# A projection's weight splits, one scan product and one group's transposes moved in the order of a hybrid decoder step

## The chip, the cores and the metric

The kernel runs on one core of one Trainium2 chip. The metric is the device time in microseconds, median over runs; lower is better. Five engines work side by side, each through its own queue in order: PE (matrix products; PEld is its weight load), DVE, ACT and POOL (element work), and SP, which issues nearly all loads.

## The reference, cut to what matters

One decoder layer for 512 prompt tokens and 8 x 8 sample tokens (576 columns), all in fp32:

```
x += 1/2 gate1 * SwiGLU1(mod(rmsnorm(x)))
h  = mod(rmsnorm(x))
x += gate2 * W_out( sum_i sigmoid(gate_i(h)) * proj_i(branch_i(h)) )
     A: dilated window attention, three head groups (dilation 1, 4, 16), merged by softmax denominators
     B: Mamba-2 scan in chunks of 128, conv, gated group norm
     C: RG-LRU with conv, block gates, GeLU side gate
x += 1/2 gate3 * SwiGLU2(mod(rmsnorm(x)));  final rmsnorm
```

Sample tokens attend to cached keys and values (4096 past positions, windows 128, 512, 2048).

## The kernel before, in words

Every dense product is done as three fp32r products of split operands: `xh*wh + xh*wl + xl*wh`, where the high part is a rounding cast (ACT) and the low part the remainder (DVE, or POOL for units made with `pool=True`). The work is a list of **units**, one per 128 output columns. `run` walks them: for each it issues loads ahead on SP (`more(room)`, room counted in products of one half), splits weights ahead on ACT and DVE/POOL (`split`), takes the finished unit before it out of PSUM (`evict`), and issues its matmuls, 24 for a unit with four k tiles and both halves of the columns. `later(n, f)` puts an instruction off by n calls of `flush`; a unit without lanes flushes twice, once at its start ahead of `evict` and once in its middle. Units whose lanes name "sk" or "sv" are `tight`: they load two units ahead at most and split one ahead. Wide tiles come from two pools with a fixed number of buffers, W (17) and B (55); a new tile takes the buffer that was given back longest ago, and its first writer waits for that buffer's last reader. PSUM has four buffers for units (`mm`) and four for everything else (`px`).

**Lanes** are generators that are stepped between a unit's matmuls, by a share per unit, and so fill in the rest: `ssd` (scan), `attn` (prompt attention and merge), `sk` and `sv` (sample keys, sample values), `lru`. A unit can also drain lanes: it runs what is left of them before its own products.

The order around the change: 16 units of branch B gates and others carry `ssd`; 36 q/k/v units carry `attn`; then 16 units of branch C (attn 7 steps a unit, sk 8, sv 4, lru 2), 11 gate units (sk 5, sv 5, lru 4), the 8 units of the C projection (c0 to c7 here: sk 2, sv 5), the 8 units of the A projection (a0 to a7; a0 drains attn, sk and sv and then splits the sample columns of the attention output, `split_o`), and `w_out` (o0 to o7 for the first half of the columns, then again for the second). a0/a1 and o0/o1 are mates: both run all but their last two k tiles first. `ev_proj` (line 2243 on) takes a projection out of PSUM: two products with the sigmoid gate (line 2248), the sum with the branches before (line 2250), and for the A projection a split of the mixed row (`split`, line 191 high on ACT, line 192 low on DVE) for `w_out`. Its gate and sum come back from DRAM (`sg`, `m`, by `ld_proj`).

The scan (`ssd`) works on 20 items (chunk, group of four heads) in a pipeline of turns: stage_a (a product `pb`, line 1387, and ACT), stage_b (ACT exponent), stage_c (line 1412, M times C.B mask on DVE; line 1415 on POOL), stage_d two turns later (products `py`), and beside them a prelude of the next chunk whose parts end in DVE products (`cbm` line 1341, `xd`, `xe` line 1355) and `state`.

Prompt attention (`pattn`) for the third group has four batches: scores (PE, line 1735; DVE adds the bias, takes the maximum), exponents (`expo`, ACT, line 1767), transposes (`transp`, PE, line 1774; copies on ACT and DVE) and `pv` (line 1791). After the three groups `pmerge` makes merge factors, sends them through DRAM (`facd`), loads them back spread out (`fx`), and then sk begins.

Of the kernel before, what the change touches and what calls it, by code (L numbers as in the profile page):

```python
# [140 lines left out]
class Kern:  # L141
# [125 lines left out]
    def run(self, units):  # L267
        nc = self.nc
        raws, wts, pss = {}, {}, {}
        nl = ns = 0  # L270
# [71 lines left out]
        seq = list(range(len(units)))  # L342
# [4 lines left out]
        at, begin = 0, {}  # L347
# [9 lines left out]
        first = self.start(ahead, split)  # L357
        ns = 2
        segs = self.segments(units, first)
        last = {g.i: n for n, g in enumerate(segs)}  # L360
        seen = 0
        for n, g in enumerate(segs):
            i, u = g.i, units[g.i]
            seen = max(seen, i)
            end = begin[seen] + size(units[seen])
            nxt = rank[min(seen + 1, len(units) - 1)]
            early = n < len(first) - 2
            tight = any(name in ("sk", "sv") for name, _ in u.lanes) or "sk" in g.drain or n < len(first)
            def more(room):
                nonlocal nl  # L370
                while nl < len(units) and begin[seq[nl]] < end + room:
                    load(seq[nl])
                    nl += 1

            if tight:
                while nl < len(units) and nl <= seen + 2 and not early:
                    load(nl)
                    nl += 1
            else:
                more(16 if isinstance(u, Pair) else 48 if nl == len(units) or isinstance(units[seq[nl]], Unit) else 32)  # L380
            while ns <= min(nxt, nl - 1) and not early:
                split(seq[ns])
                ns += 1
            self.flush()
            evict()
            for _ in range(0 if tight else 2):
                if ns < nl and begin[seq[ns]] < end + (32 if isinstance(units[seq[ns]], Unit) else 20 if isinstance(u, Unit) else 0):
                    split(seq[ns])
                    ns += 1
            for d in g.drain:  # L390
                self.drain(d)
            if g.pre is not None:
                g.pre()
            if isinstance(u, Pair):
                self.products(u, wts.pop(i), lambda n, most=7: prep(i, n, most), lambda: more(48))
                continue
            ks = u.ks()
            nk = u.w.shape[1]
            if i not in pss:
                pss[i] = {hf: self.mm() for hf in u.halves}  # L400
            (WH, WL), M, ps = wts[i], u.M, pss[i]
            kr = range(nk) if g.kr is None else g.kr
            ev = self.events(g.lanes)
            at = 0
            for q, k in enumerate(kr):
                xh, xl = ks[k]
                if any(e[2] in (id(xl), id(WL)) for e in self.todo):
                    self.flush(True)
                for p, (wt, x) in enumerate(((WH, xh), (WL, xh), (WH, xl))):
                    for hf in g.halves:  # L410
                        nc.tensor.matmul(  # L411
                            ps[hf][:M, :HALF], wt[k] if isinstance(wt, list) else wt[:, k, :], x[:, hf * HALF:(hf + 1) * HALF],
                            start=(k == 0 and p == 0), stop=(k == nk - 1 and p == 2))
                if not ev and q == len(kr) // 2:
                    self.flush()
                if g.mid is not None and q == len(kr) // 2:
                    g.mid()
                if q % 2:
                    prep(i + 2, 4, 1)
                while at < len(ev) and at * len(kr) < (q + 1) * len(ev):  # L420
                    self.flush()
                    self.step(ev[at], 1)
                    at += 1
            if last[i] == n:
                pend.append((u, pss.pop(i)))
                if i not in kept:
                    wts.pop(i)
                if u.share:
                    wts.pop(i - u.share)
# [885 lines left out]
    def ssd(self):  # L1315
# [92 lines left out]
        def stage_c(c, hg):  # L1408
            L, cs, g = (128 if c < 4 else 64), cols(c), hg // 2
            M, cv = st[c, hg]  # L1410
            four = lambda t: t.rearrange("p (h l) -> p h l", h=4)
            nc.vector.tensor_tensor(out=four(M[0:L, 0:4 * L]), in0=four(M[0:L, 0:4 * L]),
                                    in1=ctx[c][1][0:L, g * 128:g * 128 + L].unsqueeze(1).to_broadcast([L, 4, L]), op=ALU.mult)
            if c > 0:
                nc.gpsimd.tensor_tensor(out=four(cv), in0=four(cv), in1=xbc[10 + g][:, cs].unsqueeze(1).to_broadcast([128, 4, L]),
                                        op=ALU.mult)
# [20 lines left out]
        def state(c):  # L1437

            bt, cbm, xd, xe, decb, css = ctx[c]
            Sn = S[c + 1] = self.W([1024], F32, "S")  # L1440
            if c > 0:
                nc.vector.tensor_tensor(out=Sn.rearrange("p (h d) -> p h d", h=16), in0=S[c].rearrange("p (h d) -> p h d", h=16),
                                        in1=decb.unsqueeze(2).to_broadcast([128, 16, 64]), op=ALU.mult)
            for g in range(2):
                pst = self.px("pst")
                nc.tensor.matmul(pst, bt[:, g * 128:(g + 1) * 128], xe[:, g * 512:(g + 1) * 512], start=True, stop=True)
                sv = Sn[:, g * 512:(g + 1) * 512]
                if c == 0:
                    nc.scalar.copy(sv, pst)
                else:  # L1450
                    nc.vector.tensor_tensor(out=sv, in0=sv, in1=pst, op=ALU.add)
# [5 lines left out]
        for n in range(len(items) + 4):  # L1457
            if 0 <= n - 4:
                stage_d(*items[n - 4])
            if 0 <= n - 1 < len(items):  # L1460
                stage_b(*items[n - 1])
            if 0 <= n - 2 < len(items):
                stage_c(*items[n - 2])
            if n < len(items):
                c, hg = items[n]
                if hg == 0:
                    nxt = prelude(c + 1) if c < 4 else None
                    if c < 4:
                        diagonal(c + 1)
                if nxt is not None:  # L1470
                    next(nxt)
                stage_a(c, hg)
                if hg == 0 and c > 0:
                    yield
                    state(c - 1)
            yield

        for q in range(2):
# [223 lines left out]
    def pattn(self, g):  # L1702
# [99 lines left out]
                    nc.vector.tensor_copy(o.rearrange("p (i r) -> p r i", r=r), p.rearrange("p (r i) -> p r i", r=r))  # L1802
                self.po[g, j] = o

        for i in range(nb + 2):
            if 0 <= i - 1 < nb:
                transp(i - 1, 0)
            if i < nb:
                scores(i)
            if 0 <= i - 2 < nb:  # L1810
                pv(i - 2)
            yield
            if 0 <= i - 1 < nb:
                transp(i - 1, 1)
            if i < nb:
                expo(i, 0)
                expo(i, 1)
            yield
# [423 lines left out]
    def ev_proj(self, n, j, first, last):  # L2242
        def f(ps):
            nc = self.nc
            t, m = self.sg.pop((n, j))
            for hf in range(2):
                tv = t[:, hf * HALF:(hf + 1) * HALF]
                nc.vector.tensor_tensor(out=tv, in0=tv, in1=ps[hf][:, :HALF], op=ALU.mult)  # L2248
            if not first:
                nc.vector.tensor_tensor(out=t, in0=m, in1=t, op=ALU.add)  # L2250
            if last:
                self.mix[j] = self.split(t, (1, 2))
            else:
                self.store(self.md[:, j, :], t)
        return f
# [11 lines left out]
    def mixer_units(self):  # L2267
# [7 lines left out]
        u = []  # L2275
# [4 lines left out]
        def proj(w, nk, ks, n, first, last, start, drain, lanes=()):  # L2280
            for j in range(8):
                def pre(j=j):
                    if j == 0:
                        start()
                        self.ld_proj(n, 0, first)
                    if j < 7:
                        self.ld_proj(n, j + 1, first)
                    if last and j > 5:
                        self.ld_x(j - 6)

                def mid(j=j):
                    t = self.sg[n, j][0]
                    self.nc.scalar.activation(t, t, AF.Sigmoid)

                u.append(Unit(self.wview(w, 0, nk, j * 128), ks, self.ev_proj(n, j, first, last), lanes=lanes, mid=mid, pool=last,
                              pre=pre, drain=drain if j == 0 else ()))

        self.zh = {}
        for j in range(4):
# [194 lines left out]
```

## Time and profile before

| | us |
|---|---|
| median of 3 runs | 2040.97 (2040.9 to 2043.84) |
| the profiled execution | 2043.27 |
| its span, first to last instruction | 2041.3 |
| mean granted TensorE clock | 0.988 |
| busy: PE, PEld, DVE, ACT, POOL | 1976.8, 1855.3, 1230.4, 934.0, 246.4 |

The span lies 1.97 us below its execution's time, which is 2.3 us above the median. PE is busy nearly all of the time, so what can be won lies in its few idle stretches and in those that follow them.

### The profile page before, as it was taken

How to read it: one execution, taken by the hardware profiler on the slowest of the kernel's cores; microseconds unless marked ns; L12 is line 12 of the kernel's file. 1: busy time of each engine (PE TensorE's matmuls, PEld its weight loads, DVE VectorE, ACT ScalarE, POOL GpSimd, SP SyncE). 2: the span in 40 equal slices, each digit the busy share in tenths (PEclk: the TensorE clock that was granted, in tenths of full speed). 3: DMA queues.
4: the chain of work that ended last, by engine and by line, in shares of the span. 5: the costliest groups of instructions: out<-in, count | busy, mean ns of one | idle time of the engine just before them, and what ended most of it. 6: DMA issues, size and time to landing. Idle time of an engine off the chain costs nothing.

```text
span 2041.3 us, 40890 instructions
## 1 busy us (share of the span) xinstructions
PE 1976.8 (97%) x16648; PEld 1855.3 (91%) x16648; DVE 1230.4 (60%) x2463; ACT 934.0 (46%) x1885; POOL 246.4 (12%) x339
## 2 busy tenths in 40 slices
PE   7999999999999999999999989999999999999997
PEld 6779999999897899999999878888988899999997
DVE  4848677785768555225453684435345767777783
ACT  5424434356667346125352646556423743424252
POOL 2000000004004211000002131101124500000011
PEclk8999999999999999999999989999999999999998
DMA  9783223254531585332333175887877423323241
GB/s 272 262 270 115 83 83 104 83 135 155 173 102 51 169 242 167 106 111 61 87 95 98 46 248 164 283 274 239 271 247 223 155 63 104 103 80 95 78 135 55
DMA packets 374051, 300.53 MB, mean 147 GB/s; under 512 B 16304, under 2 KB 322085, under 8 KB 373864
## 3 DMA queue, kind: packets, MB, share of 16 engines
q1 hardware_dynamic: 363848, 267.48, 44.1%
q0 software_dynamic: 10016, 30.44, 4.4%
q8 instruction: 131, 2.15, 0.4%
q14 instruction: 56, 0.46, 0.1%
HBM read 266.21 MB, written 31.66 MB: 146 GB/s over the span
## 4 chain that ended last, share of the span: by engine, by line
PE 73%; DVE 10%; issue 7%; ACT 4%; DMA 3%; SPq 1%; POOL 1%; POOLq 0%; DVEq 0%; ACTq 0%
PE mm L411 46%; PE mmd L513 5%; PE mmb L513 4%; PE mmc L513 4%; PE mma L513 2%; PE kt L2019 2%; DVE op L441 2%; SPq L181 1%; PE S L2007 1%; DVE raw L441 1%; PE px_ld L776 1%; DVE wl L316 1%; PE O L2112 1%; DMA ada<-w_ada 1%; PE sc L1735 1%
## 5 line engine op out<-in xcount | busy, mean ns | idle before, releaser
L411 PE MATMUL mm<-H,wh 128*128 128x288 f32 (+1 forms) x2832 | 677.2, 309 | 5.6 <-DVE sg L2248 2.3
L411 PE MATMUL mm<-L,wh 128*128 128x288 f32 (+1 forms) x2832 | 640.2, 296 | 3.9 <-DVE L L192 2.8
L411 PE MATMUL mm<-H,wl 128*128 128x288 f32 (+1 forms) x2832 | 639.5, 296 | 1.3 <-DVE wl L316 0.8
L411 PEld LDWEIGHTS mm<-H,wh 128*128 128x128 f32 (+1 forms) x2832 | 463.6, 189 | 55.5 <-issue 41.6
L411 PEld LDWEIGHTS mm<-L,wh 128*128 128x128 f32 (+1 forms) x2832 | 466.6, 189 | 6.0 <-DVE L L192 3.9
L411 PEld LDWEIGHTS mm<-H,wl 128*128 128x128 f32 (+1 forms) x2832 | 466.4, 189 | 2.5 <-DVE wl L316 1.0
L316 DVE TENSOR_TENSOR wl<-raw,wh 128x1024 fp32r<-128x1024 f32 (+2 forms) x181 | 199.6, 1109 | 128.4 <-ACT wh L314 107.9
L447 ACT CAST op<-raw 128x512 fp32r<-128x512 f32 x228 | 135.2, 620 | 272.0 <-DVE raw L441 226.4
L314 ACT CAST wh<-raw 128x1024 fp32r<-128x1024 f32 (+2 forms) x217 | 200.6, 940 | 29.2 <-PE mm L411 21.2
L441 DVE TENSOR_TENSOR op<-raw,op 128x512 fp32r<-128x512 f32 x228 | 155.4, 686 | 26.3 <-ACT op L447 24.1
L900 DVE SCALAR_TENSOR_TENSOR x<-mm,modT,x 128x288 f32<-128x288 f32 (+1 forms) x144 | 65.0, 479 | 128.6 <-PE mm L411 128.6
L513 PE MATMUL mmd<-H,op 128*128 128x288 f32 x608 | 125.6, 299 | 1.8 <-DVE mmd L496 1.8
L513 PE MATMUL mmb<-H,op 128*128 128x288 f32 x608 | 124.0, 296 | 1.2 <-ACT su L960 1.2
L513 PE MATMUL mmc<-H,op 128*128 128x288 f32 x608 | 123.6, 296 | 0.0
L316 POOL TENSOR_TENSOR wl<-raw,wh 128x1024 fp32r<-128x1024 f32 (+2 forms) x36 | 74.9, 2091 | 401.6 <-ACT wh L314 395.1
L513 PEld LDWEIGHTS mmd<-H,op 128*128 128x128 f32 x608 | 98.5, 190 | 3.4 <-DVE mmd L496 2.3
L513 PEld LDWEIGHTS mmb<-H,op 128*128 128x128 f32 x608 | 97.5, 188 | 3.0 <-ACT su L960 2.1
L513 PEld LDWEIGHTS mmc<-H,op 128*128 128x128 f32 x608 | 97.6, 189 | 2.6 <-ACT u L526 0.8
L513 PE MATMUL mmd<-L,op 128*128 128x288 f32 x304 | 90.2, 297 | 0.0
L513 PE MATMUL mmb<-L,op 128*128 128x288 f32 x304 | 89.8, 295 | 0.0
L513 PE MATMUL mmc<-L,op 128*128 128x288 f32 x304 | 89.5, 295 | 0.0
L2024 ACT COPY KT<-kt 128x512 f32<-128x512 f32 x78 | 45.6, 588 | 75.2 <-PE kt L2019 66.9
(439 smaller groups left out, 2877.0 us busy)
## 6 DMA issues: line engine op xcount, KB each, us to landing
raw<-w_in SPq DMA_DIRECT2D x96, 512.0 KB
raw<-w_ff_in SPq DMA_DIRECT2D x88, 512.0 KB
ada<-w_ada SPq DMA_DIRECT2D x72, 512.0 KB
ck<-cache_win_kv SPq DMA_DIRECT2D x52, 512.0 KB
cv<-cache_win_kv SPq DMA_DIRECT2D x52, 512.0 KB
raw<-w_ff_out SPq DMA_DIRECT2D x60, 384.0 KB
sgd<-sg POOLq DMA_DIRECT2D x24, 288.0 KB, 4.6
sg<-sgd SPq DMA_DIRECT2D x24, 288.0 KB
```

Of the source, the lines that this page charges most:

```text
L181: self.nc.sync.dma_start(out, in_)
L314: nc.scalar.copy(H, r)
L316: self.later(0 if i < 4 else 2, lambda: e.tensor_tensor(out=L, in0=r, in1=H.bitcast(F32), op=ALU.subtract), L)
L411: nc.tensor.matmul(ps[hf][:M, :HALF], wt[k] if isinstance(wt, list) else wt[:, k, :], x[:, hf * HALF:(hf + 1) * HALF], start=(k == 0 and p ...
L441: nc.vector.tensor_tensor(out=o, in0=a, in1=b, op=op)
L447: nc.scalar.copy(ops[k][0], s)
L513: nc.tensor.matmul(banks[bank], wt[:, q, :], m, start=first and q == 0 and p == 0, stop=q == len(xs) - 1 and p == 2, skip_group_check=True)
L776: nc.tensor.matmul(ps[32 * c4:32 * c4 + 32, :], self.cT[:, k, :], r[:, q * 512:(q + 1) * 512], start=(k == 0), stop=(k == 7), skip_group_c ...
L900: nc.vector.scalar_tensor_tensor(out=x[:, c0:c0 + n], in0=ps[hf][:, 0:n], scalar=g[:, 0:1], in1=x[:, c0:c0 + n], op0=ALU.mult, op1=ALU.add)
L1735: nc.tensor.matmul(ps[hh][:, c0:c0 + 128], self.qkv["q", g, j][64 * hh:64 * hh + 64, a * 128:(a + 1) * 128], self.qkv["k", g, j][64 * hh:6 ...
L2019: nc.tensor.transpose(ps[:, j * 128:(j + 1) * 128], t[:, q, j * 128:(j + 1) * 128], self.ident)
L2024: nc.scalar.copy(kt, ps)
```

## The change

Four edits. (1) The A projection's units lose `pool=True` and get `soon = 80`: they are split through the branch of `split` that takes B buffers and puts the low parts on DVE, and `run` loads with a room of `soon + 16` (96, was 48) while the next unit to load has a `soon`, and splits with `soon` in place of 32. (2) The mixed rows' low parts are put off by 3 flushes (was 2). (3) In the scan, stage_c stands behind the prelude's part and stage_a of its turn. (4) In the third attention group transposes and `pv` run one batch later.

```diff
-                more(16 if isinstance(u, Pair) else 48 if nl == len(units) or isinstance(units[seq[nl]], Unit) else 32)
+                more(16 if isinstance(u, Pair) else units[seq[nl]].soon + 16 if nl < len(units) and units[seq[nl]].soon else 48 if nl == len(units) or isinstance(units[seq[nl]], Unit) else 32)
...
-                if ns < nl and begin[seq[ns]] < end + (32 if isinstance(units[seq[ns]], Unit) else 20 if isinstance(u, Unit) else 0):
+                if ns < nl and begin[seq[ns]] < end + (units[seq[ns]].soon or 32 if isinstance(units[seq[ns]], Unit) else 20 if isinstance(u, Unit) else 0):
...
-            if 0 <= n - 2 < len(items):
-                stage_c(*items[n - 2])
             if n < len(items):
...
                 stage_a(c, hg)
-                if hg == 0 and c > 0:
-                    yield
-                    state(c - 1)
+            if 0 <= n - 2 < len(items):
+                stage_c(*items[n - 2])
+            if n < len(items) and hg == 0 and c > 0:
+                yield
+                state(c - 1)
             yield
...
-        for i in range(nb + 2):
-            if 0 <= i - 1 < nb:
-                transp(i - 1, 0)
+        lag = 2 if g == 2 else 1
+        for i in range(nb + 1 + lag):
+            if 0 <= i - lag < nb:
+                transp(i - lag, 0)
             if i < nb:
                 scores(i)
-            if 0 <= i - 2 < nb:
-                pv(i - 2)
+            if 0 <= i - lag - 1 < nb:
+                pv(i - lag - 1)
             yield
-            if 0 <= i - 1 < nb:
-                transp(i - 1, 1)
+            if 0 <= i - lag < nb:
+                transp(i - lag, 1)
...
-                self.mix[j] = self.split(t, (1, 2))
+                self.mix[j] = self.split(t, (1, 3))
...
-                u.append(Unit(self.wview(w, 0, nk, j * 128), ks, self.ev_proj(n, j, first, last), lanes=lanes, mid=mid, pool=last,
+                u.append(Unit(self.wview(w, 0, nk, j * 128), ks, self.ev_proj(n, j, first, last), lanes=lanes, mid=mid,
                               pre=pre, drain=drain if j == 0 else ()))
+                if last:
+                    u[-1].soon = 80
```

## Rows read from the trace of the kernel before

**Rows 1.** Waits of PE, whole program: who, for whom, us, times, longest

```profile
PE kt L2019 <- DMA ck<-cache_win_kv: 8.8, 1, 8.8
PE pt L1774 <- ACT lg L1767: 2.8, 3, 1.3
```

**Rows 2.** Waits of PE in the scan, 600 to 690 us

```profile
PE pb L1387 <- DVE cbm L1341: 1.8, 2, 1.1
```

**Rows 3.** Timeline of the scan (start, us), DVE and then PE

```profile
655.31 1.71 DVE L1412 TENSOR_TENSOR M<-M,cbm 128x512 f32<-128x512 f32 x1
656.94 0.27 DVE L1341 TENSOR_TENSOR cbm<-px_cb,mats 64x128 f32<-64x128 f32 x1
...
657.27 0.50 PE L1387 MATMUL pb<-dgD,hsel 128*128 128x512 f32 x1 [1.13 <-DVE cbm L1341]
```

**Rows 4.** Timeline of PE in the third group: transposes with and without a wait

```profile
1130.78 0.60 PE L1774 MATMUL pt<-mats,lg 128*128 128x128 f32 x4
...
1140.11 1.48 PE L1774 MATMUL pt<-mats,lg 128*128 128x128 f32 x4 [1.32 <-ACT lg L1767]
```

**Rows 5.** Waits of PEld and groups of instructions, third group, 1120 to 1153 us

```profile
PEld pt L1774 <- ACT lg L1767: 6.2, 14, 1.6
...
L1767 ACT ACTIVATE lg<-lg,neg 128x128 f32<-128x128 f32 x32 | 12.4, 388 | 9.8 <-DVE neg L1758 9.8
```

**Rows 6.** Timeline of SP's queue: gate load of the third A unit

```profile
1513.34 1.62 SPq L181 DMA_DIRECT2D sg<-sgd  x1
```

**Rows 7.** Waits of PE and DVE in the A projection, 1515 to 1562 us

```profile
PE mm L411 <- DVE sg L2248: 2.3, 4, 0.7
PE mm L411 <- DVE L L192: 1.6, 1, 1.6
PE mm L411 <- DVE L L2364: 1.0, 1, 1.0
PE mm L411 <- ACT H L191: 0.8, 1, 0.8
PE mm L411 <- POOL wl L316: 0.6, 1, 0.6
...
DVE L L192 <- ACT H L191: 5.9, 8, 0.7
```

**Rows 8.** Timeline of DVE and POOL, A projection: evictions of a2, a3 and a7

```profile
1533.97 0.81 DVE L2248 TENSOR_TENSOR sg<-sg,mm 128x288 f32<-128x288 f32 x2
...
1537.81 0.81 DVE L2248 TENSOR_TENSOR sg<-sg,mm 128x288 f32<-128x288 f32 x2
1540.16 2.14 DVE L192 TENSOR_TENSOR L<-sg,H 128x576 fp32r<-128x576 f32 x1 [0.74 <-ACT H L191]
1545.89 0.76 DVE L192 TENSOR_TENSOR L<-sg,H 128x576 fp32r<-128x576 f32 x1 [0.74 <-ACT H L191]
1555.32 0.81 DVE L2248 TENSOR_TENSOR sg<-sg,mm 128x288 f32<-128x288 f32 x2
...
1538.76 5.78 POOL L316 TENSOR_TENSOR wl<-raw,wh 128x1024 fp32r<-128x1024 f32 x2 [2.98 <-ACT wh L314]
1567.76 2.40 POOL L316 TENSOR_TENSOR wl<-raw,wh 128x1024 fp32r<-128x1024 f32 x1 [1.97 <-ACT wh L314]
```

**Rows 9.** A projection's end: length; busy PE, PEld, DVE, ACT, POOL; clock; DMA; GB/s

```profile
1560.00:1564.00 4.00, 4.00 (x20) 4.00 (x20) 1.04 (x2) 1.83 (x3) 2.58 (x2) 0.57 0.43 130
1564.00:1600.00 36.00, 36.00 (x271) 35.89 (x271) 16.38 (x32) 14.53 (x24) 13.96 (x6) 1.00 0.38 107
```

**Rows 10.** Timeline of the last sample values: PE, DVE

```profile
1518.73 0.27 PE L2126 MATMUL ot<-mats,os 128*128 128x128 f32 x1
...
1519.03 0.88 DVE L2130 COPY oT<-ot 64x16 f32<-64x16 f32 x8 [3.94 <-PE ot L2126]
```

**Rows 11.** Groups of POOL by shape, 1515 to 1562 us: busy us, mean ns

```profile
L316 POOL TENSOR_TENSOR wl<-raw,wh 128x512 fp32r<-128x512 f32 x7 | 8.9, 1295 | 4.5 <-ACT wh L314 4.5
```

**Rows 12.** Page, part 5: a low part of 128x512 on DVE

```profile
L441 DVE TENSOR_TENSOR op<-raw,op 128x512 fp32r<-128x512 f32 x228 | 155.4, 686 | 26.3 <-ACT op L447 24.1
```

## The prediction

> **What bounds the kernel now.** The page comes first: PE is busy 1976.8 of 2041.3 us and the clock is nearly full, so a change can win only where PE stands idle or is held, and the list of PE's waits, whole program, says where that is. Its longest wait, 8.8 us, is for the first sample keys, and it is the end of a chain of merge factors, stores and loads that no edit shortens [rows 1]. The other views are those stretches where the diff lies, each read with the waits first and then with the timeline behind them.
>
> In the **scan** PE's `pb` waits 1.8 us in two pieces for the small mask product `cbm` [rows 2]. The timeline shows why: DVE does the 1.71 us M product just ahead of the 0.27 us `cbm`, in its order, and PE waits 1.13 us [rows 3].
>
> In the **third group** PE waits 2.8 us for exponents [rows 1]. A set of four transposes takes 0.60 us unhindered but 1.48 us behind such a wait, because its four wait one after another [rows 4]; three sets so stretched are 3 x 0.88 = 2.6 us more. So 5.4 us are seen on PE, and the weight loads' own count of the same cause is 6.2 [rows 5].
>
> In the **A projection** PE waits 2.3 + 1.6 + 1.0 + 0.8 + 0.6 = 6.3 us, mostly for DVE's evictions [rows 7]. From the eviction of a3 to that of a7 a unit takes (1555.32 - 1537.81) / 4 = 4.38 us. DVE has only 0.81 + 0.76 + 0.76 us of work for it when nothing disturbs [rows 8], but it stands 0.74 us for ACT's high part each time, 5.9 us in eight [rows 7], and the same low part takes 2.14 instead of 0.76 us when POOL's subtraction runs beside it [rows 8]. POOL's own takes 2.40 alone, and two of them 5.78 here [rows 8]. At the end of it the clock was at its lower level for a time (mean 0.57 over 4 us), after units in which PE had stood waiting; from 1564 on it is 1.00 [rows 9].
>
> **The change, part by part.**
>
> (3) *Scan.* With the M product behind `cbm`, the wait of 1.8 us goes. M's reader `py` comes two turns later, so what is late next has a turn of slack; the M product may now sit ahead of `state`'s work, and POOL's product is moved with it, with the same slack. I take -1.8; between 0, if another product of the prelude takes its place, and -1.8.
>
> (4) *Third group.* A batch of lag takes the transposes out of the exponents' shadow: 5.4 us go. What is late next: the copies of the transposes on ACT now stand behind the next batch's exponents, 12.4 / 4 = 3.1 us a batch [rows 5], and a transpose buffer of PSUM comes free only with them. Not in the trace; by those rows 0 to 3.1 us, and I take the middle, 1.5, since some copies are on DVE. So -3.9, between -6.2 (all the weight loads' wait, nothing back) and -2.3 (5.4 less 3.1). The attention lane has two more steps, so merge factors and sample keys both start two groups later; the load chain between them keeps its length and the 8.8 us stay. Other lanes find the same number of products to lie between.
>
> (2) *Put-off by 3.* The low part now comes behind the next unit's eviction, when ACT has long finished: DVE's 5.9 us of waits go [rows 7]. The mixed low parts are read only by `w_out`, units later, except the last, which o0 and o1 read only behind their other k tiles.
>
> (1) *A projection's splits.* The eight low parts of 128x512 move from POOL, 1.295 us each [rows 11], to DVE; the nearest DVE row is the same shape at 0.686 [rows 12], so 5.5 us more on DVE, early in the stretch. What hides them is DVE's idle time while a0 and a1 run their common products; if that is gone, they cost at most their 5.5 us less the 1.8 that POOL's disturbance gives back. SP: five A loads and six `w_out` loads (512 KB each) are now issued ahead of the third unit's gate loads, which were issued at 1513.34 [rows 6]. Although the number is 80, it does little else: the C units carry sample values, and such units load two ahead and split one ahead whatever the room is. So "split ahead" means a unit at most.
>
> POOL keeps `w_out`'s low parts. If it and DVE's two SBUF operations of an eviction can't run together, a unit takes 2.40 + 0.76 + 0.76 = 3.92 us [rows 8], not 4.38. Over four units that is 4 x 0.46 = 1.8, and the 0.6 us wait for POOL's `wl` goes too [rows 7]: -2.4 for (1) and (2) together. Ends: 0, and all of the waits and the slow clock, -6.3 - 1.3. (The 1.3: 20 products in 4 us against 271 / 36 x 4 = 30 [rows 9], 10 x 0.13.) I take -2.4, nearest to the rows on POOL, as these operations stay.
>
> On that the row shows 2.14 beside POOL against 0.76 alone, while products that read PSUM keep 0.81 for two [rows 8]. The Trainium skill ("Perfetto Trace Analysis", Optimizing Scalar/DVE Operations) says that GpSimd and DVE share an SBUF read port, so that moving operations between those two might not help; by that rule part (1) would give nothing, 2.4 us less than the sum. The trace agrees on the sharing; what a move gives back no row shows.
>
> (5) *What the moves push on.* The sample-key lane runs two of its steps later and so the sample-value lane ends a unit later, with its last pieces drained ahead of a0. There `ot` on PE and the copy on DVE (0.27 + 0.88 us) have nothing beside them [rows 10], and c7's eviction stands ahead of the copy. I take +1.0; between 0 and +8.8, what a cache load costs when nothing hides it [rows 1].
>
> **Sum:** -1.8 - 3.9 - 2.4 + 1.0 = -7.1 us. Behind the A projection PE has work without a gap, so the shift is carried to the end. The profiled execution, 2043.3 with 2041.3 of span, would go to 2036.2; it lies 2.3 above the median, so on the median the forecast is 2040.97 - 7.1 = **2033.9**.
>
> **The rivals.** *More.* The A projection gives up all its waits and stays at full clock, the group gives back nothing: -1.8 - 6.2 - 7.6 = -15.6, 2025.4. For it: DVE's share is only 2.33 us a unit undisturbed. Against it: POOL's subtractions remain.
>
> *No change to speak of.* PE's waits in the A projection only change their names, as DVE gets 5.5 us from POOL and the two still hold each other up; the group returns its 3.1: -1.8 - 2.3 + 1.0 = -3.1, 2037.9. It is also what the change gives if "ahead" is only a unit. The rule on the shared port named above is this case.
>
> *Slower.* The third unit's gate loads stand on SP behind six `w_out` loads, some of which need weight buffers that are free only when c7 is through, about 1519 (`ot` stands at 1518.73 [rows 10]). If then all six are moved ahead of the gate at the 107 GB/s of the stretch behind [rows 9], 3.1 MB take 29 us and the gate lands at 1548, 14 us after its eviction was at 1533.97 [rows 8]; DVE then holds the low parts queued behind it, and PE stands when its four accumulators are full. Total -1.8 - 3.9 + 1.0 + 14 = +9.3, 2050.3. It decides from the point where the gate is more than 4.7 us late. Against it: four of the six have free buffers and start earlier, and 130 GB/s were moved just before [rows 9].
>
> **How the numbers follow.** A measurement of this kernel tells 0.2%, 4.1 us, from no change. Chances: forecast 0.60 (0.02 of it within 4.1 us), more 0.12, no change 0.20, slower 0.08. So faster 0.58 + 0.12 = 0.70, the same 0.02 + 0.20 = 0.22, slower 0.08. The range leaves out "more" and "slower", 0.20 together, and takes in the rest with the bounds of the group (-6.2) and the port: 2028 to 2040.
>
> **What the profile after would show.** Right: `pb` no longer waits for `cbm`; `pt` no longer for `lg`, with sets of four at 0.60; DVE's 5.9 us for H gone and an a-unit's period under 4.0; the wait for `ck` still near 8.8; `ot` behind c7's last products. Wrong: a new wait of PE on the transposes' copies or on `px`; an A period still near 4.4; a gate load behind `w_out` loads on SP with DVE waiting for it; PE waiting for `cv` at a0; the low clock moved to another stretch instead of gone.

## The result and the profile after

The change makes the kernel slower: 2062.61 us (2061.2 to 2065.32, four runs) beside 2042.4 for the kernel before (now four runs as well), a ratio of 1.0097 with an interval of 1.008 to 1.0114. I had forecast 2033.9, a gain. The page of the profiled execution (2061.2 us) says that nothing was added to the work:

```profile
span 2059.4 us, 40905 instructions
PE 1976.5 (96%) x16648; PEld 1857.5 (90%) x16648; DVE 1231.1 (60%) x2471; ACT 933.7 (45%) x1885; POOL 238.9 (12%) x331
```

PE is busy for the same 1976.5 us (1976.8 before), so the 18 us by which the span grew are idle time. PE executes 16648 products in both, and the start of the k-th in one trace less that in the other tells where the two drift apart. The table gives that drift by stretch (times of the kernel before; plus is time lost, minus is time won, in us; the sum is the drift at the last mark; products 0, 4500, 5250, 5750, 8750, 9080, 9240, 9600, 10080, 13300 and 16640 are the marks). Kernels of the next section stand in it too.

| stretch | 4-612 | 612-698 | 698-742 | 742-1115 | 1115-1157 | 1157-1180 | 1180-1229 | 1229-1273 | 1273-1576 | 1576-2029 | sum |
|---|---|---|---|---|---|---|---|---|---|---|---|
| what lies there | | scan | | | third group | merge | first keys | first pair's softmax | samples, A projection | | |
| the change | +0.8 | -3.1 | -3.0 | 0.0 | +4.1 | +1.7 | +4.6 | +8.4 | +3.6 | +1.2 | +18.5 |
| e1, no lag | +0.2 | -3.1 | -3.0 | 0.0 | +1.1 | 0.0 | 0.0 | 0.0 | +2.6 | +1.4 | -0.9 |
| e2, lag only | +1.4 | 0.0 | -3.0 | 0.0 | +4.1 | +1.7 | +4.9 | +8.4 | -0.8 | +1.8 | +18.4 |
| e3, shift only | -1.8 | 0.0 | -3.0 | 0.0 | +1.1 | +1.7 | +6.8 | +8.4 | -0.5 | +1.1 | +13.9 |
| e4, lag without shift | +0.4 | 0.0 | -3.0 | 0.0 | +1.3 | 0.0 | 0.0 | 0.0 | +2.3 | +1.0 | +2.1 |
| e5, lag absorbed | +0.1 | -3.1 | 0.0 | 0.0 | +5.1 | 0.0 | +2.3 | 0.0 | +2.2 | +2.2 | +9.1 |
| e6, place of the values | +1.4 | +0.1 | -3.0 | 0.0 | +0.8 | +1.7 | +5.3 | +3.1 | +0.2 | +0.7 | +10.4 |
| e7, sooner | +0.8 | 0.0 | -3.0 | 0.0 | +0.8 | +1.1 | -2.6 | +6.9 | +11.9 | +0.7 | +16.6 |
| e10, w_out on DVE | +1.4 | 0.0 | -3.0 | 0.0 | +0.7 | 0.0 | +0.5 | 0.0 | -8.0 | +0.1 | -8.4 |
| e13, scan and w_out | -0.5 | -3.1 | 0.0 | 0.0 | 0.0 | 0.0 | -0.8 | 0.0 | -8.4 | -0.8 | -13.4 |
| e15, shift, early keys | +1.3 | 0.0 | -3.0 | 0.0 | +2.6 | +1.8 | -1.7 | +8.4 | 0.0 | +1.4 | +11.2 |

Two cautions. The -3.0 at 698 to 742 is no edit's: the profiled execution of before had a stretch at a lower clock there (0.66 from 725 to 735 us) that most others lack. And kernels that are alike in a stretch still differ there: by up to 2.6 us in the third group and from 1273 us on, by up to 3.5 at the first keys, and by up to 4.4 before 612 us. Clean, to 0.1 us, are 612 to 698, 742 to 1115, 1157 to 1180 and 1229 to 1273.

So the scan gave more than it should (-1.8), and the loss starts at the third group. PE's waits there, 1105 to 1160 us, to be held against [rows 1] (line numbers are each kernel's own; behind an edit they are a few higher than in the kernel before):

```profile
PE po L1791 <- DVE PT L1778: 5.2, 2, 4.2
PE pt L1774 <- ACT PT L1780: 2.4, 2, 2.1
```

The transposes no longer wait for exponents and a set of four takes 0.60 us. But 7.6 us of waits for the transposes' copies stand where 2.8 us and the stretched sets stood. DVE's timeline shows the longest:

```profile
1141.23 0.69 DVE L1778 COPY PT<-pt 128x512 f32<-128x512 f32 x1 [1.21 <-PE pt L1774]
...
1145.62 2.67 DVE L1227 SCALAR_TENSOR_TENSOR acc<-raw,v,acc 128x512 f32<-128x512 f32 x6 [0.93 <-ACT acc L1224]
...
1148.36 1.22 DVE L316 TENSOR_TENSOR wl<-raw,wh 128x1024 fp32r<-128x1024 f32 x1
1149.49 0.68 DVE L1778 COPY PT<-pt 128x512 f32<-128x512 f32 x1
```

With a batch of lag the last copy has moved past the end of a unit, and stands in DVE's queue behind that unit's eviction: a conv of 2.67 us, which first waits for ACT, and the low part of a weight. PE waits 4.17 us for it. PE's waits from 1160 to 1235 us:

```profile
PE mm L411 <- DVE wl L316: 7.4, 1, 7.4
PE S L2008 <- DVE qp L1991: 2.8, 1, 2.8
PE px_pmerge L1872 <- ACT raw L1217: 1.5, 1, 1.5
PE kt L2020 <- DVE KT L2023: 1.5, 1, 1.5
```

The 8.8 us for `ck` [rows 1] are gone from the list. In their place stand 7.4 us for a unit's low part, which is no later on DVE than before (its start is 1196.85, before 1196.97): the kernel before came to the load of the keys first and waited out the same time there. What is new at the first keys are the 2.8 us for the padded query copies (`qp`) and the 1.5 us for a key copy (`KT`) behind them. DVE's query copies wait for POOL and start later; after:

```profile
1204.33 4.40 DVE L1991 COPY qp<-qs 64x32 f32<-64x32 f32 x12 [1.60 <-POOL qp L1926]
```

and before:

```profile
1201.57 3.37 DVE L1990 COPY qp<-qs 64x32 f32<-64x32 f32 x12
```

Around these stops the granted clock is 0.76, and 0.81 in the next 8 us (the columns are those of [rows 9]):

```profile
1204.00:1212.00 8.00, 3.72 (x25) 2.97 (x24) 7.50 (x17) 1.64 (x4) 6.22 (x17) 0.76 0.69 227
```

Before, it was 1.00 in both:

```profile
1204.00:1212.00 8.00, 7.56 (x85) 6.40 (x82) 7.74 (x17) 2.71 (x5) 2.83 (x10) 1.00 0.64 190
```

From 1236 to 1285, where before has none at all, the pattern of the third group comes back:

```profile
PE kt L2020 <- DVE pp L2098: 3.9, 1, 3.9
PE S L2008 <- DVE KT L2023: 1.4, 1, 1.4
PE kt L2020 <- ACT KT L2025: 1.1, 1, 1.1
```

DVE's timeline there:

```profile
1266.83 0.48 DVE L2094 COPY pp<-ptr 128x32 f32<-128x32 f32 x4
...
1274.99 2.67 DVE L1227 SCALAR_TENSOR_TENSOR acc<-raw,v,acc 128x512 f32<-128x512 f32 x6 [4.70 <-ACT acc L1224]
...
1277.73 1.22 DVE L316 TENSOR_TENSOR wl<-raw,wh 128x1024 fp32r<-128x1024 f32 x1
1278.87 0.68 DVE L2023 COPY KT<-kt 128x512 f32<-128x512 f32 x1
1279.47 0.35 DVE L2098 COPY pp<-ptr 128x64 f32<-128x64 f32 x2
```

The last `pp` copy of the first sample pair stands behind the same block. It holds a PSUM buffer, the key transposes on PE wait for it, and in the 8 us around the end of the stop the granted clock is 0.79:

```profile
1276.00:1284.00 8.00, 4.30 (x43) 3.11 (x44) 4.49 (x11) 2.68 (x5) 0.00 (x0) 0.79 0.58 192
```

In the A projection PE's waits changed their names against [rows 7], 1515 to 1620 us:

```profile
PE mm L411 <- DVE L L192: 4.9, 3, 2.2
PE mm L411 <- DVE sg L2249: 2.1, 4, 0.7
PE mm L411 <- ACT H L2365: 0.8, 1, 0.8
PE ot L2127 <- ACT os L2123: 0.7, 1, 0.7
```

### The profile page after: what moved, and what is told of

Read it like the earlier page. It is cut to its first block, busy times and chain, and to the rows that moved or that the text cites. A ratio compares the mean times of both kernels' runs of the same rounds, so it can differ in the third digit from the quotient of the medians.

```text
span 2059.4 us, 40905 instructions
## 1 busy us (share of the span) xinstructions
PE 1976.5 (96%) x16648; PEld 1857.5 (90%) x16648; DVE 1231.1 (60%) x2471; ACT 933.7 (45%) x1885; POOL 238.9 (12%) x331
## 4 chain that ended last, share of the span: by engine, by line
PE 76%; DVE 8%; issue 5%; ACT 4%; DMA 3%; SPq 2%; POOL 1%; POOLq 0%; DVEq 0%; ACTq 0%
PE mm L411 49%; PE mmd L513 5%; PE mmb L513 4%; PE mmc L513 4%; PE mma L513 2%; PE kt L2020 2%; SPq L181 2%; DVE op L441 1%; PE S L2008 1%; PE px_ld L776 1%; PE O L2113 1%; DMA ada<-w_ada 1%; DVE raw L441 1%; DVE L L192 1%; DMA cv<-cache_win_kv 1%
## 5 line engine op out<-in xcount | busy, mean ns | idle before, releaser
L411 PE MATMUL mm<-H,wh 128*128 128x288 f32 x2768 | 662.4, 309 | 5.2 <-ACT H L701 3.0
L411 PE MATMUL mm<-H,wl 128*128 128x288 f32 x2768 | 626.8, 297 | 7.4 <-DVE wl L316 7.4
L411 PE MATMUL mm<-L,wh 128*128 128x288 f32 x2768 | 627.1, 297 | 6.2 <-DVE L L192 6.1
L411 PEld LDWEIGHTS mm<-H,wh 128*128 128x128 f32 x2768 | 453.4, 189 | 53.1 <-issue 41.1
L411 PEld LDWEIGHTS mm<-L,wh 128*128 128x128 f32 x2768 | 457.1, 189 | 8.7 <-DVE L L192 7.6
L411 PEld LDWEIGHTS mm<-H,wl 128*128 128x128 f32 x2768 | 456.9, 189 | 8.4 <-DVE wl L316 7.7
L314 ACT CAST wh<-raw 128x1024 fp32r<-128x1024 f32 (+2 forms) x209 | 195.9, 953 | 20.3 <-PE mm L411 13.1
L316 POOL TENSOR_TENSOR wl<-raw,wh 128x1024 fp32r<-128x1024 f32 (+1 forms) x28 | 64.5, 2309 | 416.1 <-ACT wh L314 406.3
```

The lines of the kernel that those rows point to most:

```text
L314: nc.scalar.copy(H, r)
L316: self.later(0 if i < 4 else 2, lambda: e.tensor_tensor(out=L, in0=r, in1=H.bitcast(F32), op=ALU.subtract), L)
L411: nc.tensor.matmul(ps[hf][:M, :HALF], wt[k] if isinstance(wt, list) else wt[:, k, :], x[:, hf * HALF:(hf + 1) * HALF], start=(k == 0 and p ...
```

## The experiments

The first ask which edit costs (e1, e2), whether it is the place in the order or the group itself (e3 to e5), and what "place" means (e6, e7); those from e8 on ask what became of the forecast gains. Each ratio is to runs of the kernel before that were taken beside the run, with its 95% interval in brackets; their medians were 2043.82 us (e1 to e4), 2044.01 (e5 to e8), 2044.49 (e9 to e12) and 2043.99 (e13 to e15).

**e1, no lag.** The change with

```diff
-        lag = 2 if g == 2 else 1
+        lag = 1
```

> Edits (1) to (3) as in the change, the third group with the lag of before. Theory (the lag costs all of it; it turns the 5 us that the change leads by at 1115 us into 18 of delay by 1440): about 2042.4 - 3 for the scan - 1 for the A projection, 2036 to 2040. Rival (the A projection's splits and SP's order cost a part that the comparison of the traces hides): 2045 or more.

Measured: 2044.64, ratio 0.9998 (0.9987 to 1.0009). The loss is gone, so it was the lag's. The gain that I expected of the rest is not there either: the scan's 3.1 us stand in the table, and by e8 below edits (1) and (2) cost about as much.

**e2, lag only.** The kernel before with edit (4).

> The kernel before with edit (4) alone. Theory: the whole loss and the other edits' gain of 3 to 4 on top, 2062 to 2068. Rival (the edits cost only together): under 2055.

Measured: 2062.06, 1.0093 (1.007 to 1.0117). The lag alone costs all of it, in the same stretches as in the change.

**e3, shift only.** The third group untouched, two empty steps behind it:

```diff
+        for _ in range(2 if g == 2 else 0):
+            yield
         for key in [k for k in self.qkv if k[1] == g]:
```

> The kernel before, its third group untouched, with two empty steps behind it, so that merge factors and sample keys come two steps later as under the change. Theory of displacement (the later place of merge, sample keys and values against the units' own work on DVE, ACT and SP is what costs): 2053 to 2062. Rival (the group itself costs: its last transposes' copies stand behind a unit's conv on DVE, and all that follows is an echo of these 4 us): 2041 to 2045.

Measured: 2057.7, 1.0069 (1.0053 to 1.0084). Two steps that do nothing cost 14 of the 20 us, with the waits of the change (7.3 for `wl`, 3.9 for `pp`).

**e4, lag without shift.** Lag of two, the first two batches' scores and exponents in one step each:

```diff
-            yield
+            if lag == 1 or i > 1:
+                yield
```

> The kernel before with the lag of two, but the first two batches' scores and exponents in one step each, so that the group has as many steps as before and nothing behind it is displaced. Theory of displacement: 2036 to 2043, the group's 5.4 us of waits mostly gone. Rival (the group itself costs): 2047 or more.

Measured: 2044.62, 1.0000 (0.9991 to 1.001), between the two ranges. Without the shift the lag costs nothing. It also wins nothing: the 2.8 us for exponents [rows 1] became 5.0 us for copies.

**e5, lag absorbed.** The whole change, with two empty steps fewer ahead of the merge factors:

```diff
-        for _ in range(5):
+        for _ in range(3):
             yield
         self.pstat_back(2)
```

> All edits of the change; two of the five empty steps ahead of the merge factors are taken out, so that the lag's two steps end there and merge, sample keys and sample values stand in the order of before. Theory (the displacement costs some 14 to 18 of the 19 us): 2042 to 2048, the group's own 3 to 5 us may stay. Rival (the lag's late copies in the group start an echo that the later order only carries on): over 2052.

Measured: 2047.25, 1.0017 (1.0006 to 1.0028). Some 16 of the 20 us come back by restoring the place of what follows (1.0097 less 1.0017). The loss in the group stays, with the copy that PE waits 4.2 us for; the profiled execution (2052.0) was the slowest of twelve, so its row in the table lies on the high side.

**e6, place of the values.** As e3, but the first pair's value lane waits one step and not two:

```diff
-            for _ in range(2):
+            for _ in range(2 if bp else 1):
                 yield
```

> The displaced kernel without lag (two empty steps behind the third group), but the first sample pair's value lane starts one step earlier, so that its copies out of PSUM (pp) stand ahead of the next unit's conv on DVE again, as before. Theory of place (a step costs where it falls behind a unit's block of evictions, conv and low part): the 7 us lost at 1243 to 1267 us go, 2049 to 2053. Rival (what costs is that everything starts later): no change, 2056 to 2060.

Measured: 2054.33, 1.0051 (1.0033 to 1.007); just outside the range, on the theory's side; by the time alone it can't be told from e3. In the stretch that it is about, one of the clean ones, 8.4 us of loss became 3.1. DVE's timeline shows the copy ahead of the block, and PE's wait for it is gone:

```profile
1268.29 0.35 DVE L2099 COPY pp<-ptr 128x64 f32<-128x64 f32 x2
...
1275.61 2.66 DVE L1227 SCALAR_TENSOR_TENSOR acc<-raw,v,acc 128x512 f32<-128x512 f32 x6 [4.16 <-ACT acc L1224]
```

**e7, sooner.** The kernel before with e5's edit alone, so everything from the merge on is two steps sooner.

> The kernel before with two of those five empty steps taken out and nothing else: merge, sample keys and values two steps sooner than before. Rival (the later, the slower): the 8.8 us wait for the first sample keys shrinks by some 2 to 3 us, 2038 to 2042. Theory of place: the sign is open, since other steps fall behind the blocks; over 2046 would speak for it, 2038 to 2042 would not tell.

Measured: 2061.84, 1.0085 (1.0069 to 1.0101). Sooner costs as much as later. The first keys do gain 2.6 us. Then DVE's order at 1240 to 1250 us is this:

```profile
1239.10 0.60 DVE L2042 TENSOR_REDUCE sst<-slg 128x1 f32<-128x432 f32 x1
...
1245.89 2.66 DVE L1227 SCALAR_TENSOR_TENSOR acc<-raw,v,acc 128x512 f32<-128x512 f32 x6 [5.88 <-ACT acc L1224]
...
1248.62 1.22 DVE L316 TENSOR_TENSOR wl<-raw,wh 128x1024 fp32r<-128x1024 f32 x1
1249.75 0.16 DVE L2047 RECIPROCAL sst<-sst 128x1 f32<-128x1 f32 x1
1250.02 0.48 DVE L2050 TENSOR_SCALAR P<-slg,sst 128x384 f32<-128x384 f32 x1
```

Now it is the softmax's own product that stands behind the block, and PE's list from 1236 to 1262 has one wait:

```profile
PE ptr L2080 <- DVE P L2051: 4.2, 1, 4.2
```

So "the later, the slower" is out. That a step behind a unit's block is what costs is shown for the 6.9 us of this stretch; 11.9 us more are lost from 1273 to 1576 us, and there I did not follow the order. PE's longest waits from 1300 to 1500 us, where before has none over 0.8, are for copies on ACT and DVE and for a gate on ACT:

```profile
PE kt L2019 <- ACT KT L2024: 2.8, 2, 2.5
PE S L2007 <- DVE KT L2022: 1.8, 1, 1.8
PE kt L2019 <- ACT gt L2176: 1.4, 1, 1.4
PE kt L2019 <- ACT pn L2099: 1.3, 1, 1.3
```

**e8, A projection only.** Edits (1) and (2) alone.

> The kernel before with edits (1) and (2) alone. My forecast: -2.4, so 2040 to 2042. From the comparison of the traces without the lag: 0 to +2, 2043 to 2046.

Measured: 2047.32, 1.0015 (1.0003 to 1.0027): no gain, rather a loss.

**e9, scan only.** Edit (3) alone.

> The kernel before with edit (3) alone. The curves of the runs with it show 3 us won between 611 and 675 us: 2039 to 2042 beside about 2043.9. Rival (the 3 us are given back at the sample keys): 2043 or more.

Measured: 2041.41, 0.9988 (0.9976 to 1.0000): a gain at the edge of what can be told, with the same 3.1 us between 612 and 698 us.

**e11, put-off only.** Edit (2) alone:

```diff
-                self.mix[j] = self.split(t, (1, 2))
+                self.mix[j] = self.split(t, (1, 3))
```

> The kernel before with edit (2) alone. My forecast's step (DVE's 5.9 us of waits go, the period falls towards 3.9): 2041 to 2043. Theory of the ring: DVE's waits go and the period stays 4.4; the last low part comes later for w_out, 2043 to 2046.

Measured: 2045.77, 1.0009 (1.0000 to 1.0019). POOL's timeline tells why nothing is won:

```profile
1536.86 5.70 POOL L316 TENSOR_TENSOR wl<-raw,wh 128x1024 fp32r<-128x1024 f32 x2 [2.98 <-ACT wh L314]
1545.54 5.70 POOL L316 TENSOR_TENSOR wl<-raw,wh 128x1024 fp32r<-128x1024 f32 x2 [2.98 <-ACT wh L314]
```

From one pair of subtractions to the next, 8.68 us for two units: 5.70 of work and 2.98 of waiting for ACT's cast, which stands behind the high part of a sum that took DVE 2.10 us while POOL ran (0.76 without). DVE's low part beside POOL, then its neighbour without:

```profile
1537.35 2.96 DVE L192 TENSOR_TENSOR L<-sg,H 128x576 fp32r<-128x576 f32 x1
...
1543.10 0.75 DVE L192 TENSOR_TENSOR L<-sg,H 128x576 fp32r<-128x576 f32 x1
```

The 0.74 us that DVE stood for ACT at each unit, 1.48 in two units, were room that this ring of POOL, ACT and DVE left. Taken away, they came back as 0.82 us more in the low part beside POOL (2.96, against 2.14 in [rows 8]) and a new stand of 0.66 for the gate's sigmoid on ACT:

```profile
1544.51 0.82 DVE L2248 TENSOR_TENSOR sg<-sg,mm 128x288 f32<-128x288 f32 x2 [0.66 <-ACT sg L2293]
```

The period is (1553.18 - 1535.82) / 4 = 4.34 us, by the starts of DVE's gate products, against 4.38 before.

**e10, w_out on DVE.** Edit (2), and the subtractions that POOL does for `w_out`, in this stretch and behind it, given to DVE:

```diff
-                self.mix[j] = self.split(t, (1, 2))
+                self.mix[j] = self.split(t, (1, 3))
...
-                              self.ev_out(j, hf), halves=(hf,), pool=True, lanes=() if hf == 0 else (("n20", 2),) + (("ada4", 1),) * (j == 2),
+                              self.ev_out(j, hf), halves=(hf,), lanes=() if hf == 0 else (("n20", 2),) + (("ada4", 1),) * (j == 2),
```

> The kernel before with edit (2) and with the low parts of w_out on DVE instead of POOL; those of the A projection stay on POOL. Theory of the ring (in the A projection POOL's two subtractions, 5.78 us, and the wait for ACT's cast between them, 2.93, set the period of two units, and DVE's stand for ACT's high part only fills it): a unit takes 3.6 us in place of 4.38, 2039 to 2042. Rival (DVE is the bound and gets 1.22 us more a unit): 2044 to 2047.

Measured: 2034.51 (2033.47 to 2035.03), 0.9952 (0.994 to 0.9965), more than the theory asked for. DVE's timeline, one unit and the start of the third after it:

```profile
1537.68 1.22 DVE L316 TENSOR_TENSOR wl<-raw,wh 128x1024 fp32r<-128x1024 f32 x1
1538.81 0.81 DVE L2248 TENSOR_TENSOR sg<-sg,mm 128x288 f32<-128x288 f32 x2
1539.66 0.76 DVE L2250 TENSOR_TENSOR sg<-m,sg 128x576 f32<-128x576 f32 x1
1540.34 0.75 DVE L192 TENSOR_TENSOR L<-sg,H 128x576 fp32r<-128x576 f32 x1
...
1548.79 0.81 DVE L2248 TENSOR_TENSOR sg<-sg,mm 128x288 f32<-128x288 f32 x2
```

In these units DVE waits for nothing, no instruction is stretched, and a unit takes (1548.79 - 1538.81) / 3 = 3.33 us. DVE took on 1.22 us a unit, and a unit got shorter by 1.05. The lower clock behind this stretch [rows 9] is gone as well:

```profile
1560.00:1564.00 4.00, 4.00 (x32) 4.00 (x31) 1.74 (x4) 0.45 (x1) 0.00 (x0) 1.00 1.16 295
```

**e12, early keys.** The first key loads and padded tiles ahead of the merge, in the kernel before:

```diff
-        yield from self.need("oT")
         qp = self.padded("qp")
...
         for i in range(2):
             ld(i)
+        yield from self.need("oT")
         yield
```

> The kernel before, with the sample keys' padded tiles and first two loads issued ahead of the merge instead of behind it. If the 8.8 us are the load's: the wait goes, up to 8 us faster, 2036 to 2040. If DVE's queue (merge products, conv, low part of the unit's weight) is the bound there, PE waits for that low part in its place as in the displaced kernels: 2042 to 2046.

Measured: 2042.5, 0.9994 (0.9984 to 1.0004). PE's list from 1180 to 1300 us has lost the 8.8 us for the load [rows 1], and got this:

```profile
PE mm L411 <- DVE wl L316: 8.4, 2, 7.3
PE S L2007 <- ACT KT L2024: 0.4, 2, 0.2
```

Behind the load stood an almost equal wait: DVE's queue of merge products, conv and low part.

Two questions stayed: whether edit (1) costs without POOL, and what makes the loss at the first keys in the displaced kernels.

**e13, scan and w_out.** e10 with edit (3).

> Edits (2) and (3) and w_out's low parts on DVE, with the A projection's on POOL and no lag. If the scan's gain and the A projection's add: 3 us below the run with w_out's low parts on DVE alone (2034.5), 2030 to 2033. If they don't: 2034 or more.

Measured: 2031.64 (2029.96 to 2037.94), 0.9947 (0.9932 to 0.9962). With e14 the fastest here. In the trace the scan's -3.1 us stand beside -8.4 in the A projection's stretch, so the two add; the step in time from e10 (0.9952) is within the noise.

**e14, edits (1) to (3) and w_out.** e1 with `w_out`'s low parts on DVE.

> The change without its lag, and w_out's low parts on DVE: the kernel of e13 with edit (1) on top. If edit (1) costs only through POOL: as e13, 2030 to 2033. If the eight low parts load DVE ahead of the first evictions, or the gates come late behind six w_out loads: 1 to 4 us more than e13.

Measured: 2032.34, 0.9946 (0.9932 to 0.9961), as e13. Edit (1) neither wins nor costs, as far as these runs can tell, once `w_out`'s subtractions are off POOL.

**e15, shift with early keys.** e3 and e12 together.

> The displaced kernel without lag, with the sample keys' padded tiles and first loads ahead of the merge. If late keys and query copies make the 6.9 us: most of them go, 2050 to 2053. If DVE's queue makes them: PE's wait for the unit's low part stays at 7 us and the time at 2055 to 2060.

Measured: 2056.04, 1.0061 (1.0045 to 1.0076). By the time, the queue of DVE; by the stretch, not so: 1180 to 1229 us lost 6.8 in e3 and gained 1.7 here, and PE's wait for the low part there is shorter:

```profile
PE mm L411 <- DVE wl L316: 5.3, 1, 5.3
```

The 8.4 us of the next stretch stay. What went from 1180 to 1229 us are the waits for the query copies and the key copy behind them, and from 1208 to 1216 us the granted clock is 1.00 here and 0.57 in e3. So by the traces the loss at the first keys is these copies' and the low clock's behind them, and the wait for the low part is not new time. The median gives back only 1.7 us of the 8.5, against an interval of some 3 us on either side; e15's row is 3.1 us worse than e3's before 612 us, ahead of both edits. How much e15 is worth in time stays open.

## Why the prediction was wrong, point by point

**The step that failed** is the one that was costed at nothing in part (4): that merge factors and sample keys both start two groups later, that the load chain between them keeps its length, and that the 8.8 us stay. The length was kept, within 1 us (from the first load of factors to the first load of keys 1174.88 to 1192.43, before 1171.43 to 1189.98); the place in the order was not, and the 8.8 us gave way to other waits. By e3 the shift alone costs 14 us; by e5 undoing it alone gives back some 16 of the change's 20. I took two steps for a delay, and a delay of a chain behind which PE has work looked free. But DVE does its instructions in the order of the program, as its timelines show. A step of a lane that falls behind the end of a unit waits for that unit's block on DVE (conv 2.67 us, low part 1.22, and DVE's own wait for ACT, up to 5.88), and PE for the step. That is shown for the group's last copy, for `pp` (e6) and for the softmax in e7; at the first keys, by the traces, it is late query copies and the clock behind them. It is a matter of places and not of lateness alone, since e7 costs 18 us for the same two steps the other way.

**The third group itself** (-3.9) was wrong in sign: +4.1 us in the table, where kernels without the lag show 0 to 1.2 (e15 2.6). The exponents' wait went as forecast. I put the copies that are late next at 1.5 us, between 0 and 3.1 by ACT's exponents; they cost 7.6 us of waits, of which 4.2 are DVE's copy behind the conv. I had looked at ACT's queue only, and the prediction names DVE's copies as relief. In e4, with the group's end where it was, gain and cost cancel.

**The scan** (-1.8) was right in mechanism and short in size: -3.1 in every run that has it, and PE's list from 600 to 690 us keeps one line.

```profile
PE py L1427 <- DVE S L1451: 0.9, 1, 0.9
```

The 1.3 us beyond the waits were not traced.

**The A projection** (-2.4) gave nothing. Of its two pieces, the put-off took DVE's 5.9 us of waits as forecast, and the period stayed (4.34 in e11), because POOL's subtractions and ACT's cast set it. I had the row, 2.14 beside POOL against 0.76 [rows 8], and even the sum 2.40 + 0.76 + 0.76 = 3.92, but with POOL's duration alone; beside DVE it takes 2.89 each, and waits 2.98 more for a cast that depends on the stretched sum: (5.78 + 2.98) / 2 = 4.38, the period that was measured. The rival "no change to speak of" had this right. And the last mixed rows' low parts, which the prediction put at nothing because o0 and o1 read them late, now come as two in 5.75 us beside POOL (e11): PE waits 4.9 us for low parts, before 1.6 [rows 7]. The Trainium skill's sentence ("Perfetto Trace Analysis", Optimizing Scalar/DVE Operations), that moving work between GpSimd and DVE might not help as they share a read port, agrees with e8, where the move gained nothing (1.0015 with it, 1.0009 in e11 without). e10 shows the other half: taking `w_out`'s subtractions off GpSimd brought 8.0 us in this stretch.

**The drain** (+1.0): `ot` waits 0.7 us for `os`, and no value load is exposed at a0 (earlier ones cost PE 1.5 us in three waits). As far as that one wait tells, it was sized right.

**The slower rival** named another place: the third unit's gate behind six `w_out` loads. SP's queue shows that very order:

```profile
1531.58 11.27 SPq L181 DMA_DIRECT2D raw<-w_out  x6
1542.91 1.50 SPq L181 DMA_DIRECT2D sg<-sgd  x1
```

The gate's load was issued 29.6 us later than before [rows 6], more than the 15 to 18 us that this kernel was late by then, and DVE stood 3.29 us for the gate's sigmoid, which ACT had waited for:

```profile
1549.48 0.82 DVE L2249 TENSOR_TENSOR sg<-sg,mm 128x288 f32<-128x288 f32 x2 [3.29 <-ACT sg L2294]
```

That is below the 4.7 us from which it was to decide. The result came out on that rival's side for another reason, and no rival named the two steps.

## What to carry to other kernels

Where lanes of small steps are woven into units on in-order queues, a change in the number of steps moves everything behind it past other instructions. Before such a step is costed at nothing, list for each moved step what stands ahead of it on DVE and ACT at the new place, above all at the ends of units; or take the steps out again elsewhere, as e5 did. And where two engines slow each other, take an engine's wait for room, not for loss, until the period of the whole ring has been worked out with the durations that they have side by side.

## What was not expected of the hardware

How much of the A projection's time went into DVE and POOL slowing each other: the same DVE instruction (128x576, both operands in SBUF) took 2.96 us beside POOL's subtraction and 0.75 without, POOL's 128x1024 subtraction 5.70 for two beside DVE and 2.40 for one alone, and DVE's own takes 1.22. And that a stop can cost beyond itself: around the ends of the 4.2 us wait in the third group and of the 3.9 us wait for `pp` the granted clock was 0.79 over 8 us each, and 1.00 in the 8 us on either side. Between levels of 1.0 and 0.5 of full speed (2.4 and 1.2 GHz) that is some 1.7 us of work lost each time, by my estimate from the 0.79.
